# State-space layer: the products on GpSimd moved to VectorE, the table of decay factors to ScalarE

## The chip, the cores and the metric

The kernel runs on one core of one Trainium2 chip. Its time is the device time of one execution in microseconds (us), the median of several runs. A profile of one more execution shows what each engine did: TensorE (PE, with its weight loads as PEld), VectorE (DVE), ScalarE (ACT), GpSimd (POOL) and SyncE (SP), which issues the DMAs.

## What is computed

The reference is one step of a two-layer model on 1280 tokens (1024 latent ones and 256 of context), 1024 wide. Layer 0 projects the normed input to q, k, v and u, runs attention on q, k, v and a bidirectional state-space layer (S5) on u, and projects both back; layer 1 is a Fourier mixer; each layer ends with a SwiGLU feed-forward part. Norms are modulated by shift, scale and gate from a conditioning vector and `w_mod`.

The change lies in S5. For each of 32 groups of 16 channels, two directions and 64 complex states it computes

```
bu = u @ (c * b)                  # complex input weights
x[t] = a * x[t-1] + bu[t]         # complex, diagonal: 64 states
y = Re(x @ c_out);  state = x[last]
```

`x` of both directions is summed into `y`, then GELU and a gated linear unit follow. The last states of the context tokens are an output too.

## The kernel before

The tokens lie along the free dimension: `CH` cuts the 1280 into chunks of 512, 512 and 256, and features lie on the partitions. Every float32 matrix is split into a high and a low part (`wsplit`, L92: a cast on ACT, L96, and a difference on POOL, L97), and a product is three matmuls of such parts (`proj3`, L114, with its matmuls in L123). The normed input is split likewise into `h` (`modulate`, L72 and L73, its differences in turn on DVE and POOL).

S5 works in blocks of eight steps: the 1280 tokens become 160 columns of eight, the recurrence runs over columns with the eighth power of `a`, and what happens inside eight steps is folded into weights. The 32 groups are taken in eight blocks `b` of four. For each block two generators run:

- `s5_prep` (L487) makes the weights. `Bs` and `Bxx` are complex products on tiles of 128x128 (`tmp` is the second product). `cmul` makes `AB` (128x512) and `CA` (128x576), each a product, a second product `ta` and their sum. PE turns `AB` into `Win`. `cpow` (L476) makes the table of rotations `E` by doubling: two products and a sum, twice, for 8, 16, 32 and 64 columns.
- `s5_main` (L562) applies them. PE multiplies `u` by `Win` (L576), ACT copies the result into `v` (L579, L581). `A` and `B` (128x648, four rows of 162) are `v` rotated by `E`, so that the scan is real: `R8` holds the decay factors and zeros where a sequence begins (mask times factor), and two scans on DVE (L596, L597) do the recurrence. Then `A` and `B` rotate back, ACT copies the sums into `x` (L608), POOL copies the last states (L609), and PE makes `y` (L622 to L624).

The helper `tt` emits the products; the profile gives them all the line of the helper: L490 in `s5_prep`, L564 in `s5_main`, L478 in `cpow`. Of the two products of each pair one is on DVE and the other, where its first argument is `G`, on POOL.

`s5_all` (L630) runs `s5_main` of a block in step with `s5_prep` of the next, eight steps per block. `build` (L1163) pulls one such step after each chunk of the projections (`pull`, L1227): four `proj3` for u (L1233), eight for q and k (L1237), then two rounds for v (L1249, matmuls L1257). It also pulls steps of `mods`, which makes the modulation of later sub-layers: 256 KB loads of `w_mod` into two buffers (L1101), matmuls (L1103), a copy on ACT (L1105), a turn on PE (L1114) and a sum on DVE (L1116). `bias_table` (L673, L674) adds small DVE work.

Each engine has one queue that runs in order. The order in the queues is set when the program is built, by a planner with its own costs that takes ready instructions by priority; it can place an instruction ahead of others that the code emits earlier. The scratch tiles of `s5_main` (tag `wm`) share six buffers, those of `s5_prep` (tag `wp`) three.

Of the kernel before, what the change touches and what calls it, by code (L numbers as in the profile page):

```python
# [5 lines left out]
AF=mybir.ActivationFunctionType; ALU=mybir.AluOpType  # L6
# [5 lines left out]
def bank(k,name="p",tag="p"):  # L12
    return k.psum.tile([128,512],F32,tag=tag,bufs=k.banks[tag],name=name)
# [51 lines left out]

def modulate(k, c, A, S, hi, lo, at):
    nc=k.nc; V=nc.vector; c0,n=CH[c]
    for kt in range(KT):
        t=at(n); x=k.xT[kt][:,c0:c0+n]
        if kt%3==1: nc.scalar.activation(t,x,AF.Identity,bias=S(kt,c),scale=A(kt,c))  # L70
        else: V.tensor_scalar(t,x,A(kt,c),S(kt,c),op0=ALU.mult,op1=ALU.add)
        nc.scalar.copy(hi[:,kt],t)  # L72
        (nc.gpsimd if kt%2 else V).tensor_tensor(out=lo[:,kt],in0=t,in1=hi[:,kt],op=ALU.subtract)  # L73

def modnorm(k, c, R, A, S, hi, lo, at):
    nc=k.nc; c0,n=CH[c]
    for kt in range(KT):
        t=at(n)
        if kt%8 in (1,2,4,5,7):
            nc.vector.tensor_tensor(out=t,in0=k.xT[kt][:,c0:c0+n],in1=R,op=ALU.mult)  # L80
            nc.scalar.activation(t,t,AF.Identity,bias=S(kt,c),scale=A(kt,c)); nc.scalar.copy(hi[:,kt],t)
            nc.gpsimd.tensor_tensor(out=lo[:,kt],in0=t,in1=hi[:,kt],op=ALU.subtract)
        else:
            nc.vector.scalar_tensor_tensor(out=t,in0=k.xT[kt][:,c0:c0+n],scalar=A(kt,c),in1=R,op0=ALU.mult,op1=ALU.mult)
            nc.scalar.activation(hi[:,kt],t,AF.Identity,bias=S(kt,c))
            nc.vector.scalar_tensor_tensor(out=lo[:,kt],in0=t,scalar=S(kt,c),in1=hi[:,kt],op0=ALU.add,op1=ALU.subtract)
# [315 lines left out]
LC=162  # L402
# [73 lines left out]
def cpow(e1,e2,re,im,tmp,ms,n):  # L476

    def tt(e,o,i,j,op): e.tensor_tensor(out=o,in0=i,in1=j,op=op)  # L478
    for m in ms:
        br=re[:,:,m:m+1].to_broadcast([128,n,m]); bi=im[:,:,m:m+1].to_broadcast([128,n,m])  # L480
        o=slice(m+1,2*m+1); i=slice(1,m+1); v=tmp[:,:,0:m]
        tt(e2,re[:,:,o],re[:,:,i],br,ALU.mult); tt(e1,v,im[:,:,i],bi,ALU.mult)
        tt(e1,re[:,:,o],re[:,:,o],v,ALU.subtract)
        tt(e2,im[:,:,o],re[:,:,i],bi,ALU.mult); tt(e1,v,im[:,:,i],br,ALU.mult)
        tt(e1,im[:,:,o],im[:,:,o],v,ALU.add)

def s5_prep(k, b, P, io, res):  # L487

    nc=k.nc; V=nc.vector; G=nc.gpsimd; S=nc.scalar
    def tt(e,o,i,j,op): e.tensor_tensor(out=o,in0=i,in1=j,op=op)  # L490
    wt=lambda name,tag="wp",n=3: k.s5b.tile([128,4,LC],F32,tag=tag,bufs=n,name=name)
    xt=lambda sh,name: k.x.tile(sh,F32,tag="x",bufs=8,name=name)
    sm=lambda sh,name,n=1: k.s5b.tile(sh,F32,tag=name,bufs=n,name=name)
    bc=sm([128,4,2,4,16],"bc"); nc.sync.dma_start(bc,io["BC"][b])
    Bst,Bx,Cst,Cx=[bc[:,i] for i in range(4)]
    dd=sm([128,16],"dd"); nc.sync.dma_start(dd,io["dd"][b//2,:,b%2])
    UT=xt([128,1152],"UT"); U=UT[:,0:640].rearrange("p (g c) -> p g c",g=4); Toep=UT[:,640:1152].rearrange("p (g c) -> p g c",g=4)
    gs=lambda t,d: t[:,d*32+4*b:d*32+4*b+4]
    Bs=sm([128,2,5,16],"Bs"); Bxx=sm([128,2,4,16],"Bxx"); tmp=sm([128,2,4,16],"tmp")
    V.memset(Bs[:,:,4],0.0)  # L500
    g2=lambda t: t.rearrange("p (d g) -> p d g",d=2)[:,:,4*b:4*b+4][:,:,:,None].to_broadcast([128,2,4,16])
    tt(V,Bs[:,:,0:4],Bst,g2(P["cr"]),ALU.mult); tt(G,tmp,Bx,g2(P["ci"]),ALU.mult); tt(V,Bs[:,:,0:4],Bs[:,:,0:4],tmp,ALU.add)
    tt(V,Bxx,Bx,g2(P["cr"]),ALU.mult); tmp=sm([128,2,4,16],"tmp"); tt(G,tmp,Bst,g2(P["cn"]),ALU.mult); tt(V,Bxx,Bxx,tmp,ALU.add)
    V.tensor_scalar(Bxx,Bxx,io["sgn"],None,op0=ALU.mult)
    V.tensor_scalar(Cst,Cst,io["sgn"],-1.0,op0=ALU.mult,op1=ALU.mult)
    V.tensor_scalar(Cx,Cx,-1.0,None,op0=ALU.mult)
    yield
    def cmul(o,d,n,sl,u,v):
        p=lambda t: gs(t,d)[:,:,sl][:,:,:,None].to_broadcast([128,4,n,16])
        bb=lambda t: t[:,:,None,:].to_broadcast([128,4,n,16])  # L510
        ta=wt("ta").rearrange("p a c -> p (a c)")[:,0:64*n].rearrange("p (a j h) -> p a j h",a=4,h=16)
        tt(V,o,p(P["PR"]),bb(u),ALU.mult)
        tt(G,ta,p(P["PI"]),bb(v),ALU.mult)
        tt(V,o,o,ta,ALU.add)
    Win=xt([128,2,4,128],"Win"); CA=xt([128,2,4,9,16],"CA")
    def turn(d,AB):
        p=bank(k,tag="s").rearrange("p (a b) -> p a b",a=4)
        for i in range(4): nc.tensor.transpose(p[:,i],AB[:,i].rearrange("p h j -> p (h j)"),k.ident)
        S.copy(Win[:,d],p)
    old=None  # L520
    for d in range(2):

        AB=wt("AB").rearrange("p a c -> p (a c)")[:,0:512].rearrange("p (a h j) -> p a h j",a=4,h=16)
        cmul(AB.rearrange("p a h j -> p a j h"),d,8,slice(0,8) if d==0 else slice(7,None,-1),Bs[:,d,0:4],Bxx[:,d])
        yield
        cmul(CA[:,d],d,9,slice(0,9) if d==0 else slice(8,None,-1),Cst[:,d],Cx[:,d])
        if old is not None: turn(d-1,old)
        old=AB
        yield
    turn(1,old)  # L530

    p=bank(k,tag="s")[:,0:256].rearrange("p (a c) -> p a c",a=2)
    for d in range(2):
        for g in range(4):
            rhs=CA[:,0,g,0:8] if d==0 else CA[:,1,g,1:9]
            nc.tensor.matmul(p[32*g:32*g+32,d],lhsT=Bs[:,d].rearrange("p g h -> p (g h)")[:,16*g:16*g+32],rhs=rhs.rearrange("p j h -> p (j h)"),start=True,stop=True)
    KT=sm([128,15,16],"KT")
    S.copy(KT[:,7:15],p[:,0].rearrange("p (j h) -> p j h",h=16))
    S.copy(KT[:,0:7],p[:,1].rearrange("p (j h) -> p j h",h=16)[:,0:7])
    tt(V,dd,dd,KT[:,7],ALU.add)  # L540
    tt(V,KT[:,7],p[:,1].rearrange("p (j h) -> p j h",h=16)[:,7],dd,ALU.add)
    kd=io["kt_dr"][b]
    nc.sync.dma_start(kd,KT.rearrange("p j h -> p (j h)"))
    for g in range(4):
        a=kd[32*g:32*g+16]
        nc.sync.dma_start(Toep[:,g],bass.AP(tensor=a.tensor,offset=a.offset,ap=[[240,16],[16,8],[1,128]]))
    yield

    E=[wt(f"E{i}","E",4) for i in range(2)]
    ep=P["e"].rearrange("p i (d q) c -> p i d q c",d=2)[:,:,:,2*b:2*b+2]  # L550
    for i in range(2): V.tensor_copy(dq(E[i])[:,:,:,0:9],ep[:,i])
    t=wt("t")
    cpow(V,V,E[0],E[1],t,(8,16),4)
    yield
    cpow(V,G,E[0],E[1],t,(32,64),4)
    for i in range(2): G.tensor_copy(E[i][:,:,129:162],E[i][:,:,0:33])
    res[b]=(Win,CA,U,Toep,E)
    yield

def dq(t): return t.rearrange("p (d q) c -> p d q c",d=2)  # L560

def s5_main(k, b, P, io, res):  # L562
    nc=k.nc; V=nc.vector; G=nc.gpsimd; S=nc.scalar
    def tt(e,o,i,j,op): e.tensor_tensor(out=o,in0=i,in1=j,op=op)  # L564
    wt=lambda name: k.s5b.tile([128,4,LC],F32,tag="wm",bufs=6,name=name)
    Win,CA,U,Toep,E=res.pop(b)
    nc.sync.dma_start(U,io["u_dr"][64*b:64*b+64].rearrange("(g h) s c -> (h s) g c",g=4))
    Vr=[]
    for ri in range(2):
        v=wt("v")  # L570
        for d in range(2):
            p=bank(k,tag="s")
# [10 lines left out]
        Vr.append(v)  # L583
    yield
    R8=wt("R8"); A=wt("A"); B=wt("B")
    r8=P["r8"].rearrange("p (d q) -> p d q",d=2)[:,:,2*b:2*b+2][:,:,:,None].to_broadcast([128,2,2,LC])
    tt(G,dq(R8),k.s5mask[:,None,None,:].to_broadcast([128,2,2,LC]),r8,ALU.mult)
    C,Sn=E
    tt(V,A,Vr[0],C,ALU.mult); tt(G,B,Vr[1],Sn,ALU.mult)
    tt(V,A,A,B,ALU.add)  # L590
    tt(V,B,Vr[1],C,ALU.mult); tt(G,Vr[0],Vr[0],Sn,ALU.mult)
    tt(V,B,B,Vr[0],ALU.subtract)
    for i,t in enumerate((A,B)): V.tensor_copy(dq(t)[:,:,:,0:1],io["s0"][:,i,:,2*b:2*b+2][:,:,:,None])
    yield
# [5 lines left out]
    def put(ri,op):  # L600
# [6 lines left out]
                else: oa,ob=xo[:,:,127::-1],xo[:,:,159:127:-1]  # L607
                S.copy(oa,A[h,q,0:128]); S.copy(ob,A[h,q,129:161])  # L608
        G.tensor_copy(fin[:,ri,:,2*b:2*b+2][:,:,:,None],dq(A)[:,:,:,161:162])  # L609
    tt(V,A,Vr[0],C,ALU.mult); tt(G,B,Vr[1],Sn,ALU.mult)  # L610
    put(0,ALU.subtract)
    yield
    A=wt("A"); B=wt("B"); tt(V,A,Vr[1],C,ALU.mult); tt(G,B,Vr[0],Sn,ALU.mult)
    put(1,ALU.add)
    yield
    yield
# [1 line left out]
    for g0 in (0,2):  # L618
        p=bank(k,tag="s")[:,0:320].rearrange("p (a b) -> p a b",a=2)
# [10 lines left out]
def s5_all(k, P, io):  # L630

    res={}
    for _ in s5_prep(k,0,P,io,res): yield
    for b in range(8):
        m=s5_main(k,b,P,io,res); p=s5_prep(k,b+1,P,io,res) if b<7 else iter(())
        for _ in range(8):
            next(m,None); next(p,None)
            yield
# [808 lines left out]
```

## Time and profile before

| what | before |
|---|---|
| median of 3 runs | 3035.34 us (3032.78 to 3039.38) |
| the profiled execution | 3033.56 us, its span 3031.8 us |
| PE busy | 2709.9 us (89%) |
| DVE busy | 1985.8 us (65%) |
| ACT busy | 1142.1 us (38%) |
| POOL busy | 1065.4 us (35%) |
| DMA | 391.71 MB, 129 GB/s on average |
| granted PE clock over the span | 0.944 |

Busy shares are averages over stages with different limits. S5 runs in the first 15% of the span; its stage is read from views of that stretch. A wait is put down to the instruction that released it last, and a wait of PE stands twice in the profile, at the matmul and at its weight load.

### The profile page before, as it was taken

How to read it: one execution, taken by the hardware profiler on the slowest of the kernel's cores; microseconds unless marked ns; L12 is line 12 of the kernel's file. 1: busy time of each engine (PE TensorE's matmuls, PEld its weight loads, DVE VectorE, ACT ScalarE, POOL GpSimd, SP SyncE). 2: the span in 40 equal slices, each digit the busy share in tenths (PEclk: the TensorE clock that was granted, in tenths of full speed). 3: DMA queues.
4: the chain of work that ended last, by engine and by line, in shares of the span. 5: the costliest groups of instructions: out<-in, count | busy, mean ns of one | idle time of the engine just before them, and what ended most of it. 6: DMA issues, size and time to landing. Idle time of an engine off the chain costs nothing. (4 is left out here: it accounts for less than half of the span.)

```text
span 3031.8 us, 49180 instructions
## 1 busy us (share of the span) xinstructions
PE 2709.9 (89%) x18042; PEld 2471.6 (82%) x18042; DVE 1985.8 (65%) x3769; ACT 1142.1 (38%) x2419; POOL 1065.4 (35%) x913
## 2 busy tenths in 40 slices
PE   4778889888998999999999997996799999989997
PEld 1556666766797999999999986985699999989996
DVE  8876740787668766564667748377947454666674
ACT  3332332565445333333422223244433333443232
POOL 3665534554224311111433344343411111243334
PEclk7888999999998999999999998997899999999998
DMA  6245567344433333333643432431323332554421
GB/s 223 84 121 154 162 189 212 82 117 117 158 106 116 102 128 121 120 134 112 222 140 132 143 107 70 153 106 56 120 82 130 117 114 88 168 198 154 159 79 70
DMA packets 283706, 391.71 MB, mean 129 GB/s; under 512 B 34236, under 2 KB 196156, under 8 KB 283464
## 3 DMA queue, kind: packets, MB, share of 16 engines
q1 hardware_dynamic: 265320, 330.74, 34.1%
q10 hardware_dynamic: 15552, 53.09, 5.1%
q0 software_dynamic: 2592, 4.73, 0.6%
q8 instruction: 142, 2.33, 0.3%
q14 instruction: 100, 0.82, 0.1%
HBM read 291.96 MB, written 96.50 MB: 128 GB/s over the span
## 5 line engine op out<-in xcount | busy, mean ns | idle before, releaser
L276 PE MATMUL p<-op,w 128*128 128x320 f32 x8688 | 1342.9, 315 | 83.5 <-ACT w L160 24.0
L276 PEld LDWEIGHTS p<-op,w 128*128 128x128 f32 x8688 | 1312.2, 192 | 105.0 <-ACT w L160 26.9
L160 POOL TENSOR_TENSOR w<-raw,w 128x512 fp32r<-128x512 f32 (+1 forms) x230 | 321.4, 1400 | 973.8 <-ACT w L160 902.2
L160 ACT CAST w<-raw 128x512 fp32r<-128x512 f32 (+1 forms) x396 | 240.0, 607 | 283.8 <-PE p L276 182.6
L276 PE MATMUL p<-op,e 128*128 128x320 f32 x1728 | 274.3, 312 | 16.4 <-ACT e L160 11.4
L276 PEld LDWEIGHTS p<-op,e 128*128 128x128 f32 x1728 | 258.3, 189 | 22.8 <-ACT e L160 11.9
L177 DVE TENSOR_TENSOR raw<-raw 128x512 f32<-128x512 f32 (+1 forms) x228 | 159.4, 699 | 165.5 <-POOL w L160 104.5
L320 DVE SCALAR_TENSOR_TENSOR xt<-p,mod,xt 128x320 f32<-128x320 f32 (+2 forms) x432 | 193.4, 471 | 101.4 <-PE p L276 99.7
L283 DVE TENSOR_TENSOR e<-p,e 128x320 f32<-128x320 f32 x264 | 127.0, 486 | 168.3 <-PE p L276 144.0
L160 DVE TENSOR_TENSOR w<-raw,w 128x512 fp32r<-128x512 f32 (+1 forms) x166 | 123.3, 743 | 120.5 <-ACT w L160 117.6
L123 PE MATMUL p<-h,wh 128*128 128x512 f32 (+1 forms) x576 | 185.8, 394 | 18.0 <-ACT h L72 11.6
L160 POOL TENSOR_TENSOR e<-raw,e 128x384 fp32r<-128x384 f32 x72 | 79.0, 1097 | 260.2 <-ACT e L160 260.2
L123 PEld LDWEIGHTS p<-h,wh 128*128 128x128 f32 x576 | 109.0, 201 | 49.9 <-ACT h L72 12.7
L1348 PE MATMUL p<-o,w 128*128 128x320 f32 x768 | 115.6, 312 | 3.6 <-ACT w L160 3.6
L1348 PEld LDWEIGHTS p<-o,w 128*128 128x128 f32 x768 | 114.6, 191 | 4.0 <-ACT w L160 3.8
L160 ACT CAST e<-raw 128x384 fp32r<-128x384 f32 x96 | 48.7, 512 | 179.9 <-PE p L276 113.6
L309 DVE TENSOR_TENSOR e<-e 128x320 f32<-128x320 f32 (+1 forms) x216 | 110.1, 561 | 0.8 <-DMA hT<-e 0.4
L123 PE MATMUL p<-h,wl 128*128 128x512 f32 (+1 forms) x288 | 110.5, 384 | 0.0
L767 POOL TENSOR_TENSOR P<-P,l 128x384 f32<-128x384 f32 (+1 forms) x80 | 68.7, 860 | 104.4 <-DVE l L764 65.1
L332 DVE TENSOR_TENSOR op<-op 128x320 fp32r<-128x320 f32 x120 | 84.1, 726 | 16.9 <-ACT op L332 16.9
L160 ACT CAST w<-st 128x512 fp32r<-128x512 f32 (+1 forms) x76 | 44.6, 587 | 132.0 <-PE p L276 129.6
L103 PE MATMUL p<-ac 128*128 128x512 f32 (+1 forms) x432 | 92.0, 367 | 2.3 <-DVE ac L380 2.3
(397 smaller groups left out, 4520.6 us busy)
## 6 DMA issues: line engine op xcount, KB each, us to landing
hT<-e SPq DMA_DIRECT2D x324, 160.0 KB
op<-hT ACTq DMA_DIRECT2D x108, 480.0 KB
mw<-in_w_mod_dram SPq DMA_DIRECT2D x160, 256.0 KB
raw<-in_wg_dram SPq DMA_DIRECT2D x104, 256.0 KB
raw<-in_wu_dram SPq DMA_DIRECT2D x104, 256.0 KB
raw<-in_wd_dram SPq DMA_DIRECT2D x96, 192.0 KB
xt<-x_dr SPq DMA_DIRECT2D x24, 640.0 KB
xt<-in_x_dram SPq DMA_DIRECT2D x16, 640.0 KB
```

The lines of the kernel that those rows point to most:

```text
L103: k.nc.tensor.matmul(p,lhsT=w,rhs=x,start=i==0,stop=i==n-1)
L123: k.nc.tensor.matmul(ps[c],lhsT=w[i][:,kt],rhs=h[c][j][:,4*pc+kt],start=pc==0 and kt==0 and m==0,stop=pc==1 and kt==3 and m==2)
L160: k.nc.scalar.copy(hi,src); eng.tensor_tensor(out=lo,in0=src,in1=hi,op=ALU.subtract)
L177: def tt(o,x,y,op=ALU.subtract): V.tensor_tensor(out=o,in0=x,in1=y,op=op)
L276: k.nc.tensor.matmul(p,lhsT=w[i][:,kt],rhs=x[j][:,kt],start=P in (1,2,5) and n==0,stop=n==3*kn-1,skip_group_check=P!=2); n+=1
L283: def add(o): V.tensor_tensor(out=o,in0=p,in1=o,op=ALU.add)
L309: def tt(o,x,y): V.tensor_tensor(out=o,in0=x,in1=y,op=ALU.subtract)
L320: x=k.xT[d][:,c0:c0+n]; V.scalar_tensor_tensor(out=x,in0=p[:,o:o+n],scalar=self.gate(d,c),in1=x,op0=ALU.mult,op1=ALU.add)
L332: nc.scalar.copy(hi,r); (nc.vector if self.nq%3 else nc.gpsimd).tensor_tensor(out=lo,in0=r,in1=hi,op=ALU.subtract)
L767: nc.gpsimd.tensor_tensor(out=a,in0=a,in1=l.to_broadcast(a.shape),op=ALU.mult)
L1348: nc.tensor.matmul(ps[r],lhsT=w[x][:,kt],rhs=o[t][y][:,4*pc+kt,HALF*r:HALF*r+HALF],start=pc==0 and kt==0 and n==0,stop=pc==1 and kt==3 and ...
```

## The change

All products and sums of two operands in S5 go to DVE. `R8` is no longer one product on POOL over 128x648: for each of its four rows ACT scales the mask (162 elements) by that row's factor. The copies of `E` and of the last states and the memsets stay on POOL, as does everything outside S5.

```diff
--- before.py
+++ after.py
@@ -499,8 +499,8 @@
-    tt(V,Bs[:,:,0:4],Bst,g2(P["cr"]),ALU.mult); tt(G,tmp,Bx,g2(P["ci"]),ALU.mult); tt(V,Bs[:,:,0:4],Bs[:,:,0:4],tmp,ALU.add)
-    tt(V,Bxx,Bx,g2(P["cr"]),ALU.mult); tmp=sm([128,2,4,16],"tmp"); tt(G,tmp,Bst,g2(P["cn"]),ALU.mult); tt(V,Bxx,Bxx,tmp,ALU.add)
+    tt(V,Bs[:,:,0:4],Bst,g2(P["cr"]),ALU.mult); tt(V,tmp,Bx,g2(P["ci"]),ALU.mult); tt(V,Bs[:,:,0:4],Bs[:,:,0:4],tmp,ALU.add)
+    tt(V,Bxx,Bx,g2(P["cr"]),ALU.mult); tmp=sm([128,2,4,16],"tmp"); tt(V,tmp,Bst,g2(P["cn"]),ALU.mult); tt(V,Bxx,Bxx,tmp,ALU.add)
@@ -510,7 +510,7 @@
         tt(V,o,p(P["PR"]),bb(u),ALU.mult)
-        tt(G,ta,p(P["PI"]),bb(v),ALU.mult)
+        tt(V,ta,p(P["PI"]),bb(v),ALU.mult)
         tt(V,o,o,ta,ALU.add)
@@ -552,7 +552,7 @@
-    cpow(V,G,E[0],E[1],t,(32,64),4)
+    cpow(V,V,E[0],E[1],t,(32,64),4)
@@ -583,12 +583,13 @@
     R8=wt("R8"); A=wt("A"); B=wt("B")
-    r8=P["r8"].rearrange("p (d q) -> p d q",d=2)[:,:,2*b:2*b+2][:,:,:,None].to_broadcast([128,2,2,LC])
-    tt(G,dq(R8),k.s5mask[:,None,None,:].to_broadcast([128,2,2,LC]),r8,ALU.mult)
+    r8=P["r8"].rearrange("p (d q) -> p d q",d=2)[:,:,2*b:2*b+2][:,:,:,None]
+    for d in range(2):
+        for q in range(2): S.activation(R8[:,2*d+q],k.s5mask,AF.Copy,scale=r8[:,d,q])
     C,Sn=E
-    tt(V,A,Vr[0],C,ALU.mult); tt(G,B,Vr[1],Sn,ALU.mult)
+    tt(V,A,Vr[0],C,ALU.mult); tt(V,B,Vr[1],Sn,ALU.mult)
     tt(V,A,A,B,ALU.add)
-    tt(V,B,Vr[1],C,ALU.mult); tt(G,Vr[0],Vr[0],Sn,ALU.mult)
+    tt(V,B,Vr[1],C,ALU.mult); tt(V,Vr[0],Vr[0],Sn,ALU.mult)
     tt(V,B,B,Vr[0],ALU.subtract)
@@ -607,10 +608,10 @@
-    tt(V,A,Vr[0],C,ALU.mult); tt(G,B,Vr[1],Sn,ALU.mult)
+    tt(V,A,Vr[0],C,ALU.mult); tt(V,B,Vr[1],Sn,ALU.mult)
     put(0,ALU.subtract)
     yield
-    A=wt("A"); B=wt("B"); tt(V,A,Vr[1],C,ALU.mult); tt(G,B,Vr[0],Sn,ALU.mult)
+    A=wt("A"); B=wt("B"); tt(V,A,Vr[1],C,ALU.mult); tt(V,B,Vr[0],Sn,ALU.mult)
     put(1,ALU.add)
```

## Rows read from the trace of the kernel before

**Rows 1.** Windows: stretch, length; busy (count) of PE, PEld, DVE, ACT, POOL; clock, DMA.
```profile
66.00:220.00 154.00, 112.36 (x687) 85.80 (x687) 125.50 (x197) 52.20 (x137) 100.43 (x92) 0.84 0.34 97
220.00:455.00 235.00, 203.69 (x1584) 147.77 (x1582) 151.58 (x260) 75.87 (x212) 115.50 (x128) 0.92 0.57 168
455.00:525.00 70.00, 66.28 (x371) 46.62 (x371) 7.09 (x11) 17.60 (x22) 29.70 (x25) 1.00 0.70 201
```
**Rows 2.** Waits of PE from 66 to 220 us: total us, times, longest.
```profile
PE p L623 <- ACT x L608: 18.5, 2, 12.1
...
PE p L1103 <- DVE mod L1116: 7.4, 1, 7.4
```
**Rows 3.** Waits of PE from 220 to 455 us.
```profile
PE p L1103 <- DMA mw<-in_w_mod_dram: 15.6, 12, 3.5
PE p L1103 <- DVE mod L1116: 5.2, 2, 2.8
PE p L1103 <- ACT mr L1105: 4.5, 1, 4.5
PE p L1114 <- ACT mr L1105: 3.5, 2, 2.3
```
**Rows 4.** Windows right after six stalls of PE: the first and the last of six.
```profile
146.40:151.00 4.60, 4.60 (x17) 4.31 (x18) 3.39 (x19) 3.66 (x11) 1.32 (x6) 0.53 0.45 139
...
437.00:441.00 4.00, 4.00 (x31) 3.78 (x32) 0.00 (x0) 3.65 (x2) 0.00 (x0) 0.57 0.66 209
```
**Rows 5.** Groups by line on POOL, 58 to 450 us: busy, mean ns | idle before.
```profile
L564 POOL TENSOR_TENSOR B<-v,E 128x648 f32<-128x648 f32 x24 | 46.6, 1950 | 34.8 <-DVE v L597 34.8
...
L97 POOL TENSOR_TENSOR wl<-raw,wh 128x512 fp32r<-128x512 f32 x26 | 39.1, 1507 | 34.3 <-ACT wh L96 32.0 <-DVE Bs L490 2.3
...
L490 POOL TENSOR_TENSOR tmp<-bc,s5ci 128x128 f32<-128x128 f32 x8 | 4.5, 556 | 9.4 <-DMA bc<-in_BC_dram 9.4
```
**Rows 6.** Timeline of POOL: start us, duration us, what.
```profile
269.25 1.37 POOL L97 TENSOR_TENSOR wl<-raw,wh 128x512 fp32r<-128x512 f32 x1 [0.54 <-ACT wh L96]
```
**Rows 7.** Timeline of DVE at the same time.
```profile
269.42 1.25 DVE L478 TENSOR_TENSOR t<-E 128x32 f32<-128x32 f32 x1
270.59 0.18 DVE L478 TENSOR_TENSOR E<-E 128x32 f32<-128x32 f32 x1
```
**Rows 8.** Lines L490 and L564 on DVE: shortest/median/longest ns, first and last start us.
```profile
L490 DVE TENSOR_TENSOR AB<-s5PR,Bs x16: 1065/1910/2312, 73.0 to 373.1; 128x512 f32<-128x512 f32 x16
...
L490 DVE TENSOR_TENSOR CA<-s5PR,bc x16: 743/746/751, 93.1 to 393.2; 128x576 f32<-128x576 f32 x16
...
L564 DVE TENSOR_TENSOR B<-v,E x8: 810/834/835, 132.2 to 422.7; 128x648 f32<-128x648 f32 x8
```
**Rows 9.** Timeline of DVE: products of `cpow` with POOL idle or elsewhere.
```profile
228.08 0.29 DVE L478 TENSOR_TENSOR t<-E 128x128 f32<-128x128 f32 x1
...
229.77 0.42 DVE L478 TENSOR_TENSOR t<-E 128x256 f32<-128x256 f32 x1
```
**Rows 10.** Groups by line on DVE, 66 to 455 us.
```profile
L564 DVE TENSOR_TENSOR A<-A,B 128x648 f32<-128x648 f32 x24 | 33.6, 1418 | 33.1 <-POOL B L564 33.1
L564 DVE TENSOR_TENSOR A<-v,E 128x648 f32<-128x648 f32 x24 | 28.5, 1211 | 29.8 <-ACT v L581 29.8
L490 DVE TENSOR_TENSOR AB<-s5PR,Bs 128x512 f32<-128x512 f32 x16 | 26.3, 1643 | 0.3
L490 DVE TENSOR_TENSOR AB<-AB,ta 128x512 f32<-128x512 f32 x16 | 25.9, 1622 | 7.8 <-POOL ta L490 7.8
...
L596 DVE TENSOR_TENSOR_SCAN v<-R,A 128x648 f32<-128x648 f32 x8 | 12.0, 1498 | 0.0
```
**Rows 11.** Timeline of DVE: first and last piece of one block's scan part.
```profile
246.58 0.83 DVE L564 TENSOR_TENSOR A<-v,E 128x648 f32<-128x648 f32 x1 [5.39 <-ACT v L581]
...
260.75 2.94 DVE L564 TENSOR_TENSOR A<-A,B 128x648 f32<-128x648 f32 x2 [1.47 <-POOL B L564]
```
**Rows 12.** Groups by line on ACT, 58 to 450 us.
```profile
L608 ACT COPY x<-A 64x256 f32<-64x256 f32 (+1 forms) x128 | 35.3, 322 | 73.3 <-DVE A L564 72.4
```

## The prediction

> **What bounds the kernel now.** I read the page first: the chain that ended last lies in the feed-forward part, but it reaches back only to the second half of the span, so it says nothing about the stage that is changed. The state-space layer (S5) is found by its lines, L490, L478 and L564, which run from about 70 to 430 us [rows 8]. Next I read the windows by stage [rows 1]. From 66 to 220 us VectorE (DVE) is busy for 125.5 of 154 us and TensorE (PE) for 112.4 at a granted clock of 0.84. From 220 to 455 us PE is busy for 204 of 235 us and DVE for 152. Behind them, from 455 us, PE is busy for 66 of 70 us at full clock, so what PE wins before 455 us is passed on.
>
> Then the waits of PE. Up to 220 us, 18.5 us are spent at L623, the S5 output product, whose x copies ScalarE (ACT) makes from a DVE sum, and 7.4 us on L1116, a small DVE sum of the modulation that stands in DVE's queue among S5's [rows 2]. After 220 us there are 5.2 us on the same L1116 and 4.5 + 3.5 us on L1105, an ACT copy behind those x copies; 15.6 us are spent on the loads of w_mod [rows 3]. S5 therefore holds PE for 25.9 + 13.2 = 39.1 us.
>
> [...]
>
> **Why S5 is late.** Its products are split over DVE and GpSimd (POOL). POOL needs 1.95 us on average for a product of 128x648 [rows 5], DVE 0.83 where nothing disturbs it [rows 8]. And the two do not really run side by side. POOL's L97 ran from 269.25 to 270.62 us [rows 6]; the DVE product of 128x32 that starts at 269.42 takes 1.25 us and ends at 270.67, right behind it, while the next one of that size takes 0.18 [rows 7]. A DVE operation on two SBUF tensors was held until the POOL operation had ended.
>
> **The change, step by step.** Nine groups of POOL instructions go; the largest is B with 46.6 us, the smallest tmp (ci) with 4.5 [rows 5]; the nine sum to 148.1 us, nearly all of it in the first two windows, in which POOL is busy for 216 [rows 1]. L97's 39.1 us stay, with the h split, memsets and small copies.
>
> Added on DVE, 112 instructions in eight blocks: 32 products of 128x648 at 0.834 (B<-v,E is the same operation, already on DVE) make 26.7 us; 16 of 128x576 at 0.746 make 11.9 [rows 8]; 16 of 128x512 have no undisturbed row with these layouts: below, 0.66 by scaling the 576 one, above, 1.07, the least of AB, which writes across its tile; ta is written in order, so I take 0.66, 10.6 us (17.1 at most) [rows 8]; 32 of 128x128 at 0.29, 9.3 us, and 16 of 128x256 at 0.42, 6.7 us [rows 9]. Together 65.2 us as durations.
>
> Neighbours overlap a little: the operation that ends at 270.67 us has its follower starting at 270.59 [rows 7]. With 0.08 us off each of 112 the queue grows by 56 us, of which 3.0 per block lie in the scan part (s5_main) and 4.0 in the preparation. [...]
>
> Removed from DVE's time: waits for POOL's result, 33.1 us in front of A<-A,B and 7.8 in front of AB<-AB,ta; and holding. Over their undisturbed durations [rows 8] the four largest groups spend 33.6 - 20.0, 28.5 - 20.0, 26.3 - 17.1 and 25.9 - 17.1 us, together 40.3 [rows 10]. Two thirds of POOL's time leaves (148 of 216), so I let two thirds of this go, 27 us; none of it is the lower bound, and all of it, with smaller groups that I don't count, the upper.
>
> Per block, scan part: + 3.0 - 33.1/8 - (22.1 x 2/3)/8 = + 3.0 - 4.1 - 1.8 = - 2.9 us. A single block shows the same: from the first A at 246.58 to the end of the last sum at 263.69 us it takes 17.1 us [rows 11]; twelve operations of 0.834, two scans of 1.5 [rows 10] and two small copies (0.1 each by the starts in rows 7) make 13.2, so - 3.9. Preparation: + 4.0 - 7.8/8 - (18.2 x 2/3)/8 = + 4.0 - 1.0 - 1.5 = + 1.5 us.
>
> R8, the decay table, becomes four ACT instructions per block of 162 elements. The nearest row is ACT's copy, 0.32 us [rows 12]: 32 x 0.32 = 10.3 us on ACT, which spends 72 us waiting for DVE's A. It is needed only at the scan, seven DVE operations later. I cost it at nothing; if ACT's queue brings it late, 1.3 us per block, 10 in all, is the other end.
>
> What hides the rest. After 220 us DVE has 83 us idle, so the preparation's + 1.5 is covered and only the scan part counts: five blocks at 2.9 to 3.9 us make 14.5 to 19.5, and PE can gain there at most its S5 stalls of 13.2 and half the clock loss, 7.2, together 20.4. I take 16. Before 220 us DVE is busy for four fifths of the time and has little cover, so both parts count: three blocks at - 1.4 make 4, and with some clock given back 6. The sum is - 22 us. Bounds: 0 if nothing of the holding goes and ACT is late, - 54 (39.1 + 14.5) if every S5 stall ends.
>
> POOL's queue gets shorter, and L97 no longer stands behind products that wait for DVE, so the weight splits come earlier. Next late in the second stretch are the w_mod loads, two buffers deep.
>
> The profiled execution took 3033.56 us (span 3031.8), 1.8 below the median of 3035.34. 3033.6 - 22 = 3011.6, on the median's scale 3013 us.
>
> **Rivals.** (A) All S5 stalls end, because the remaining lateness falls under PE's other work. For it: the 18.5 us at L623 are two stalls only [rows 2]. Against it: before 220 us DVE is near full. 3035.3 - 54 = 2981 us.
>
> (B) No change: PE reaches each w_mod product earlier and waits there instead. For it: 15.6 us of such waits, and loads that can't be issued before PE has read the buffer. Against it: they are spread over twelve waits, and DMA is at 0.57 [rows 1, 3]. 3031 to 3039 us.
>
> (C) Slower: DVE becomes the bound. The mechanism is that the long DVE durations don't come from the moved POOL work (L97, DMA or layout cause them) and stay. Then + 65.2 - 41 = + 24 us on a queue which is full up to 220 us and on which L1116 and the h splits of the first projection wait too: 3059 us. It decides from the point where the holding that goes is less than 15 us (56 - 41). For it: part of the holding is L97's. Against it: the pair of rows 6 and 7, where the same size takes 1.25 and 0.18 us.
>
> The order in the queues is a planner's, made at build: L1116 stands among S5's work, though that is emitted elsewhere. With other operations it may place S5's products at other points of PE's queue; that is part of each case's width.
>
> **Chances.** Forecast, 2990 to 3027 us: 0.62. (A) 0.16. (B) 0.10. (C) 0.12. From a measured kernel 0.2% (6 us) is about what can be told from no change. Faster 0.78, same 0.10, slower 0.12. The range takes in (A) and (B) and leaves out (C): 2979 to 3038 us.
>
> **What would show it.** A<-A,B at a mean near 0.85 us instead of 1.42 and no DVE wait for POOL at L564; AB near 1.1; DVE's busy time up to 455 us about the same as now, with less idle time; PE's wait at L623 below 10 us and the clock from 66 to 220 us above 0.86; the w_v products (L1257) starting some 20 us earlier than at 455 us; everything behind them equally long. Wrong would be: A<-A,B still above 1.2 us; an L623 wait that grows; or a later stage whose length changes by more than a few us.

## The result, and the profile after

The changed kernel takes 2998.55 us (median of 4 runs, 2994.13 to 3000.1), the kernel before on the same chip 3035.3 us: ratio 0.9879, 95% interval 0.9867 to 0.9891. That is 36.8 us less, where 22 were forecast. The profiled execution took 2994.13 us, its span is 2992.4 us. One run of e5 below (3725.86 us) and one of the kernel before that was timed beside it (5654.81 us) took far longer than the others and are left out of every comparison. Lines behind `R8` stand one further down than before (L608 is now L609).

Where the time went is read at the landmark that the prediction chose, the first weight load of the w_v products, which ends S5's stretch. The rows, of before and of after, give the first and the last start.

```profile
L1257 PEld LDWEIGHTS p<-wh,h x160: 186/188/192, 455.5 to 522.6; 128*128 128x128 f32 x160
```

```profile
L1258 PEld LDWEIGHTS p<-wh,h x160: 186/188/192, 411.1 to 479.1; 128*128 128x128 f32 x160
```

The stretch got 44.4 us shorter. Windows of before over it, and up to 250 us:

```profile
66.00:250.00 184.00, 138.82 (x900) 105.17 (x904) 144.10 (x238) 61.58 (x165) 115.74 (x113) 0.84 0.37 105
...
66.00:455.50 389.50, 316.37 (x2276) 233.75 (x2276) 277.08 (x457) 128.07 (x349) 216.43 (x219) 0.89 0.48 140
```

And of after, over the same work and over the two stages of [rows 1]:

```profile
66.00:220.00 154.00, 134.37 (x896) 101.42 (x896) 142.88 (x293) 66.09 (x181) 56.22 (x53) 0.92 0.42 120
220.00:455.00 235.00, 212.75 (x1642) 148.29 (x1637) 137.54 (x282) 83.05 (x213) 63.90 (x58) 0.96 0.66 194
```

```profile
66.00:411.10 345.10, 305.51 (x2257) 222.76 (x2258) 276.45 (x566) 134.16 (x377) 104.76 (x99) 0.93 0.53 153
```

Three things are to be seen. PE's idle time in the stretch fell from 389.5 - 316.4 = 73.1 us to 345.1 - 305.5 = 39.6, by 33.5; its busy time for nearly the same matmuls (2257 against 2276 records) fell by 10.9, with the granted clock up from 0.89 to 0.93. The two make the 44.4. DVE's busy time did not move, 277.1 and 276.5 us, though 109 more instructions ran on it. And the lead was won early: by 220 us PE has started 896 matmuls, which it had reached only by 250 us before (900). Busy time times clock, as an estimate of the work, says the same: 134.4 x 0.92 = 124 against 138.8 x 0.84 = 117.

The waits of PE, first from 66 to 220 us and then to 411 us, answer to [rows 2, 3].

```profile
PE p L1104 <- DMA mw<-in_w_mod_dram: 4.4, 3, 2.9
...
PE p L623 <- ACT Win L519: 2.8, 1, 2.8
PE p L1104 <- DVE mod L1117: 2.8, 1, 2.8
```

```profile
PE p L1104 <- DMA mw<-in_w_mod_dram: 9.3, 16, 1.3
PE p L123 <- POOL wl L97: 7.8, 2, 4.9
PE p L624 <- ACT x L609: 1.1, 1, 1.1
```

The products that waited for the x copies, L623 before, are L624 now; what is L623 now was L622. So the 18.5 us on the x copies are gone up to 220 us, and 1.1 us are left behind it; the loads of w_mod cost 13.7 us in place of 15.6, and one wait is new: 7.8 us on L97, the low half of the weights on POOL.

DVE's groups up to 440 us (they answer to [rows 10]):

```profile
L564 DVE TENSOR_TENSOR B<-v,E 128x648 f32<-128x648 f32 x32 | 29.6, 924 | 2.2 <-ACT v L581 2.1
L564 DVE TENSOR_TENSOR A<-A,B 128x648 f32<-128x648 f32 x24 | 21.8, 908 | 0.1
L564 DVE TENSOR_TENSOR A<-v,E 128x648 f32<-128x648 f32 x24 | 20.6, 860 | 12.2 <-ACT v L581 12.2
L490 DVE TENSOR_TENSOR AB<-s5PR,Bs 128x512 f32<-128x512 f32 x16 | 19.9, 1246 | 0.1
L490 DVE TENSOR_TENSOR AB<-AB,ta 128x512 f32<-128x512 f32 x16 | 19.1, 1195 | 0.0
L478 DVE TENSOR_TENSOR E<-E,t 128x32 f32<-128x32 f32 (+3 forms) x64 | 18.6, 291 | 0.0
```

No group waits for POOL any more, and A<-A,B went from a mean of 1.42 to 0.91 us. The two largest groups that are left on POOL:

```profile
L97 POOL TENSOR_TENSOR wl<-raw,wh 128x512 fp32r<-128x512 f32 x32 | 61.5, 1924 | 173.0 <-ACT wh L96 162.6 <-PE p L1104 10.2 <-DMA UT<-u_dr 0.2
L610 POOL COPY fin<-A 128x4 f32<-128x4 f32 x16 | 27.8, 1759 | 59.5 <-DVE A L564 59.5
```

The second of these groups in the kernel before, from 58 to 450 us, and then the decay table after:

```profile
L609 POOL COPY fin<-A 128x4 f32<-128x4 f32 x16 | 10.1, 629 | 7.1 <-DVE A L564 7.0
```

```profile
L588 ACT ACTIVATE R<-mk,s5r 128x162 f32<-128x162 f32 x32 | 12.4, 442 | 0.0
```

L97 takes 1.92 us where it took 1.51 [rows 5], and a copy of four columns 1.76 where it took 0.63: what stays on POOL became slower. Behind S5 about 5 us are given back in the profiled executions (spans of 3031.8 and 2992.4 us, 39.4 of the 44.4; by the medians 36.8). The attention that follows starts at 480.8 instead of 524.3 us and ends at 747.3 instead of 786.5: 4.3 us longer.

```profile
L754 PE MATMUL S<-ch,qs x64: 393/497/795, 524.3 to 786.5; 128*128 128x512 f32 x64
```

```profile
L755 PE MATMUL S<-ch,qs x64: 392/497/794, 480.8 to 747.3; 128*128 128x512 f32 x64
```

### The profile page after: what moved, and what is told of

Same layout as the page of the kernel before. It is cut to its first block, busy times and chain, and to the rows that moved or that the text cites. A ratio compares the mean times of both kernels' runs of the same rounds, so it can differ in the third digit from the quotient of the medians.

```text
span 2992.4 us, 49124 instructions
## 1 busy us (share of the span) xinstructions
PE 2698.2 (90%) x18042; PEld 2463.3 (82%) x18042; DVE 1985.4 (66%) x3881; ACT 1151.3 (38%) x2451; POOL 951.0 (32%) x793
## 5 line engine op out<-in xcount | busy, mean ns | idle before, releaser
L97 POOL TENSOR_TENSOR wl<-raw,wh 128x512 fp32r<-128x512 f32 x44 | 77.0, 1752 | 201.0 <-ACT wh L96 190.6
```

The source lines that it names most:

```text
L97: nc.gpsimd.tensor_tensor(out=l,in0=raw,in1=h,op=ALU.subtract)
```

## The experiments

All are timed against the kernel before on their own chip. "S5's end" is the first start of the w_v loads, as above.

| run | what | median us | ratio to before, 95% | S5's end |
|---|---|---|---|---|
| after | the change | 2998.55 | 0.9867 to 0.9891 | 411.1 |
| e1_lock | after + unread POOL products | 3058.04 | 1.0049 to 1.0095 | 475.5 |
| e2_write | after + POOL memsets | 3011.65 | 0.9890 to 0.9947 | 430.4 |
| e3_main | scan part alone | 3003.92 | 0.9868 to 0.9920 | 422.9 |
| e4_prep | preparation alone | 3029.49 | 0.9970 to 0.9993 | 443.9 |
| e5_fin_dve | after, fin on DVE | 2995.10 | 0.9844 to 0.9881 | 404.9 |
| e6_fin_act | after, fin on ACT | 2977.53 | 0.9793 to 0.9824 | 394.6 |
| e7_r8_pool | after, R8 on POOL | 2989.67 | 0.9826 to 0.9862 | 402.2 |
| e8_after_again | after, with e5 to e7 | 2992.58 | 0.9847 to 0.9884 | 409.6 |
| e9_fin_act_r8_pool | e6 and e7 together | 2982.95 | 0.9798 to 0.9846 | 402.9 |
| e10_low_on_dve | e6 + 24 of L97 on DVE | 2984.72 | 0.9804 to 0.9851 | 397.6 |

**Does POOL's reading hold DVE?** The theory has two parts. A hand-off is DVE's wait for a result of POOL; holding is the longer time that a DVE operation takes while POOL runs. The two kernels give back to POOL about the time that the change took from it, in work whose result (`k.jk`, a scratch half of a tile) nobody reads. In the first it reads two SBUF inputs. In the second it writes: 117 us of memsets, with one product of four elements ahead of each row (24, together 16 us). DVE and PE have the work of the kernel after, in the same numbers and in the same order. `caf` is a view of the tile `CA`, `jf` one of a table of `E`.

```diff
 # e1: in s5_prep, twice per block, and in s5_main, once per block
...
+        for _ in range(3): tt(G,k.jk,caf[64:128,d,0:512],caf[64:128,d,0:512],ALU.mult)
...
+    for _ in range(6): tt(G,k.jk,jf(C),jf(Sn),ALU.mult)
 # e2: at the same places
...
+        tt(G,k.jk[:,0:4],caf[64:128,d,0:4],caf[64:128,d,0:4],ALU.mult)
+        for _ in range(7): G.memset(k.jk,0.0)
...
+    tt(G,k.jk[:,0:4],jf(C)[:,0:4],jf(Sn)[:,0:4],ALU.mult)
+    for _ in range(14): G.memset(k.jk,0.0)
...
```

> The changed kernel with 96 extra products on POOL (64 partitions x 512, six in each scan part and six in each preparation) whose results nobody reads; the output is unchanged, and the queues of PE, DVE and ACT stand in the same order as in the changed kernel. Holding (a POOL operation that reads SBUF holds DVE's two-input operations): POOL gets about 100 us of work back, A<-A,B on DVE rises from 0.91 us to 1.2 or more, and 20 to 30 of the 36.8 us are given back: 3018 to 3030 us. Hand-off (the gain came from waits for POOL's slower half of each pair, which is not restored here): no more than 3003 us. Order (the planner's other order made the gain; it is kept here): no more than 3003 us.

> The same as the first, but POOL's extra work is 224 memsets that only write SBUF (each row of them behind one product of four elements), again read by nobody and with the queues of PE, DVE and ACT in the same order. If only POOL operations that read SBUF hold DVE: A<-A,B stays near 0.91 us and the time at 2996 to 3004 us. If any POOL operation does, or if POOL's full queue (L97 behind the extra work) is what costs: as in the first, 3015 us or more. Hand-off and order: no more than 3003 us.

Windows of the first and of the second, from 66 us to S5's end:

```profile
66.00:475.50 409.50, 317.31 (x2257) 230.88 (x2258) 348.59 (x567) 134.50 (x377) 249.01 (x195) 0.89 0.44 128
```

```profile
66.00:430.40 364.40, 306.81 (x2258) 224.11 (x2259) 276.66 (x566) 134.40 (x377) 241.62 (x347) 0.92 0.50 145
```

POOL is busy for 144 and 137 us longer than after (104.8). With the reading, DVE needs 72.1 us more for the same instructions; with the writing, 0.2. So about half a microsecond of DVE is lost per microsecond of the added reading, and next to none for the writing. The groups show it at the instruction (E<-E,t had 0.29 and A<-A,B 0.91 us), again the first and the second:

```profile
L478 DVE TENSOR_TENSOR E<-E,t 128x32 f32<-128x32 f32 (+3 forms) x64 | 34.1, 533 | 0.0
...
L566 DVE TENSOR_TENSOR A<-A,B 128x648 f32<-128x648 f32 x24 | 26.1, 1087 | 0.1
```

```profile
L567 DVE TENSOR_TENSOR A<-A,B 128x648 f32<-128x648 f32 x24 | 21.8, 910 | 0.1
...
L478 DVE TENSOR_TENSOR E<-E,t 128x32 f32<-128x32 f32 (+3 forms) x64 | 20.0, 312 | 0.1
```

The reading costs more than the change gained, 59.5 us over the kernel after where 20 to 30 were expected, with next to no hand-off (DVE waits 2.7 us for POOL in it). A<-A,B came to 1.09 us only, short of the 1.2 expected; the small products of `E` lost more, E<-E,t alone 15.5 us. The theory of the holding is confirmed; hand-offs or another order alone don't explain the gain. With the hand-offs gone, the order kept and POOL reading again, S5 ends at 475.5 us, 20 us later than before the change.

The writing came out between its two expectations, 13 us above the kernel after, and costs in another way. L97 comes later behind the memsets in POOL's queue (12.1 us of PE's waits in place of 7.8), and PE waits 16.2 us in two places for loads of `UT`. These are late through L97 as well. In SyncE's queue a load of weights (L94) waited until L97 had read the buffer, 57.7 us in nine waits; both late loads of `UT` stand right behind such an L94, the first issued at 119.40 us, 0.9 us after an L94 that had waited 6.3 us. SyncE's waits for L97 up to S5's end, with the memsets and in the kernel after:

```profile
SPq L94 <- POOL wl L97: 57.7, 9, 18.1
```

```profile
SPq L94 <- POOL wl L97: 29.2, 8, 13.9
```

The profile of e2 is of its longest run (3019.8 us), so its S5's end stands at the late side.

**Which part?** The scan part alone and the preparation alone, on the kernel before. The planner's order of PE's queue is another one in each of them.

```diff
 # e3: s5_main as after; s5_prep as before
-    tt(V,A,Vr[0],C,ALU.mult); tt(G,B,Vr[1],Sn,ALU.mult)
+    tt(V,A,Vr[0],C,ALU.mult); tt(V,B,Vr[1],Sn,ALU.mult)
...
 # e4: s5_prep as after; s5_main as before
-        tt(G,ta,p(P["PI"]),bb(v),ALU.mult)
+        tt(V,ta,p(P["PI"]),bb(v),ALU.mult)
...
```

> One part of the change alone: s5_main's products on DVE and its table on ACT, the preparation as before. By the working of the prediction this part shortens a block by 2.9 us and more and the preparation lengthens it by 1.5: 3005 to 3012 us, that is at least two thirds of the 36.8. If holding is what counts, POOL keeps 75 us of the preparation's work and AB's mean on DVE stays above 1.4 us. If the preparation's share is the larger one: above 3020 us.

> The other part alone: the preparation's products on DVE, s5_main as before with its waits for B on POOL. By the prediction's step (+1.5 us per block): 3033 to 3042 us. By holding, which frees the preparation's DVE operations, and if the two parts add up: 36.8 less what the main part gives, 3020 to 3030 us.

S5's end comes 32.6 us earlier with the scan part, 11.6 with the preparation; together that is 44.2, as with both (44.4). Per block they are worth 4.1 and 1.5 us. Of the total, 30 us are the scan part's, whose time lies 1 us below its range, and 5 the preparation's, in the range by holding, whose kernel gives back 4.4 us in the attention. Each leaves the other's contention standing; first a group of the scan part alone, then one of the preparation alone:

```profile
L490 DVE TENSOR_TENSOR AB<-AB,ta 128x512 f32<-128x512 f32 x16 | 25.8, 1610 | 10.2 <-POOL ta L490 10.2
```

```profile
L564 DVE TENSOR_TENSOR A<-A,B 128x648 f32<-128x648 f32 x24 | 37.2, 1568 | 18.7 <-POOL B L564 18.7
```

**What is next late?** The new wait on L97 and the copies of `fin`, which stand ahead of it in POOL's queue, led to these four. The last is the kernel after once more.

```diff
 # e5, e6: fin on DVE, on ACT
-        G.tensor_copy(fin[:,ri,:,2*b:2*b+2][:,:,:,None],dq(A)[:,:,:,161:162])
+        V.tensor_copy(fin[:,ri,:,2*b:2*b+2][:,:,:,None],dq(A)[:,:,:,161:162])
+        S.copy(fin[:,ri,:,2*b:2*b+2][:,:,:,None],dq(A)[:,:,:,161:162])
 # e7: the table back on POOL
...
-        for q in range(2): S.activation(R8[:,2*d+q],k.s5mask,AF.Copy,scale=r8[:,d,q])
+    tt(G,dq(R8),k.s5mask[:,None,None,:].to_broadcast([128,2,2,LC]),r8,ALU.mult)
```

> The kernel after, with the copy of the last column of each part (fin) on VectorE in place of GpSimd. In the kernel after these 16 copies hold GpSimd's in-order queue for 27.8 us and keep it waiting for VectorE's A for 59.5 us, and the low half of the weights (L97) is queued behind them: TensorE waits 7.8 us for it, in 2 places. Theory (the end of GpSimd's queue is the next bound): both waits go, 16 copies of some 0.1 to 0.3 us come to VectorE, and it runs 3 to 8 us below the kernel after: 2990 to 2996. Rival (the two waits are made up by matmuls that the planner has in hand): 2997 to 3002, no difference.

> The same copy on ScalarE in place of GpSimd. Theory (the wait for VectorE's A, not the copy, is what costs): the wait of 59.5 us moves into ScalarE's in-order queue, ahead of the modulation, the evictions and the high half of the weights, so TensorE's waits on ScalarE grow: 3000 to 3012. Rival (ScalarE is waiting for that A anyway, because its next instruction is the copy of x that reads the same A): as with the copy on VectorE, 2990 to 2998.

> The kernel after, with the table of decay factors back on GpSimd (8 instructions of 128x648) in place of 32 small ones on ScalarE. Theory (it was off the path; what it holds of VectorE is 8 times at most its own 1.5 us): 0 to 8 us above the kernel after, 2998 to 3006. Rival (ScalarE's 12.4 us for it stood on the path, ahead of the copy of v for which VectorE waits 12.2 us): 3 to 10 us below the kernel after, 2988 to 2995.

> The kernel after as it stands, on the same chip as the three kernels above, to compare them with: 2994 to 3002 by what it took the first time. If it comes out elsewhere, the three are compared with this run and not with the first.

With fin on DVE the time does not move (2995.10 beside 2992.58, whose runs reach from 2991 to 3002). My theory of POOL's queue is not borne out: the fin copies are gone from POOL, yet PE still waits 4.0 us for L97 (8.4 in e8), and the 4.7 us by which S5 ends earlier don't show in the total. The timelines tell why L97 is late without them. First after, around the longer of its two stalls: POOL from 380.06 us, DVE's row of products at that time, and PE.

```profile
380.06 7.50 POOL L97 TENSOR_TENSOR wl<-raw,wh 128x512 fp32r<-128x512 f32 x2 [22.23 <-ACT wh L96]
...
383.04 0.82 DVE L564 TENSOR_TENSOR A<-A,B 128x648 f32<-128x648 f32 x1
383.78 0.82 DVE L564 TENSOR_TENSOR B<-v,E 128x648 f32<-128x648 f32 x1
384.63 1.79 DVE L564 TENSOR_TENSOR A<-A,B 128x648 f32<-128x648 f32 x1
385.78 0.79 PE L123 MATMUL p<-h,wl 128*128 128x512 f32 x1 [4.89 <-POOL wl L97]
```

Then the kernel with fin on DVE, where no fin copy is ahead of L97 either:

```profile
327.65 4.15 POOL L97 TENSOR_TENSOR wl<-raw,wh 128x512 fp32r<-128x512 f32 x1 [17.50 <-ACT wh L96]
```

Two L97, whose median is 1.30 us, take 7.5, one takes 4.15. DVE's products ran back to back at 0.82 us, undisturbed, for as long as L97 stood, until one took 1.79. By these rows the holding went both ways: a DVE queue without gaps kept POOL out. After this stall the clock was low: 0.50 from 386 to 391 us of the kernel after.

With fin on ACT the time falls by 15 us, to 2977.53, the best of all and below both expectations. The 16 copies take 0.197 us each there, and ACT does not pay for the wait: it is idle for 0.3 us before them, and for 28.5 us before the x copies of the same `A`, where it was 31.7 in the kernel after. But the copy itself is worth little (DVE did it in 0.30). What differs is the stretch from 295 to 400 us; first fin on ACT, then the kernel after run beside it:

```profile
295.00:400.00 105.00, 97.81 (x791) 70.15 (x791) 65.09 (x128) 45.12 (x122) 21.92 (x21) 1.00 0.68 203
```

```profile
295.00:400.00 105.00, 89.35 (x695) 64.82 (x694) 66.26 (x129) 34.91 (x107) 34.72 (x26) 0.90 0.58 169
```

PE's wait for L97 is 1.0 us here instead of 8.4, and the clock stays at 1.00. A shorter queue on POOL is not what it takes. With the table back on POOL (e7) POOL is busy for 112.0 us up to S5's end, in e8 for 107.4, and PE waits only 0.8 us for L97; with both edits (e9) it does not wait for L97 at all. Both end S5 at 402 to 403 us, some 8 us behind fin on ACT. So that wait is not all of the 15 us. The planner's order of PE's queue differs in every variant (e5, e6, e7, e9, e10; e8 has that of the kernel after); what the order is worth was not tested and stays open. The table back on POOL takes 2989.67, in its rival's range, but its runs overlap with those of the kernel after: no difference can be told.

**Do they add up, and does the remaining contention cost anything?** Two more: both edits together, and fin on ACT with the low half of the weights of u, q and k on DVE.

```diff
 # e10, on top of fin on ACT: proj3 hands DVE to the helper for the difference
-    nc.gpsimd.tensor_tensor(out=l,in0=raw,in1=h,op=ALU.subtract)
+    (low or nc.gpsimd).tensor_tensor(out=l,in0=raw,in1=h,op=ALU.subtract)
```

> The kernel after with fin on ScalarE and the table of decay factors back on GpSimd, the two edits that each came out below it alone (by 15 and by 3 us). If each takes away its own cost, they add up: 2970 to 2977. Rival (both worked through the same stall, TensorE's wait for the low weights of L97, or through the order that the planner then chose): nothing is added, 2976 to 2990.

> The kernel with fin on ScalarE (2977.5 us), and in the projections of u, q and k the low half of the weights (L97, 24 instructions of 128x512) on VectorE too in place of GpSimd. Theory (VectorE and GpSimd hold each other: L97 takes 1.93 us on average where it needs 1.28, and VectorE waits behind it): 24 products of 0.7 us are added to VectorE, 17 us, and the holding that L97 causes goes, about as much, so its products come down to their undisturbed durations (the 128x32 ones of E to 0.18) and the time stays within 2970 to 2980. Rival (VectorE is full up to 220 us and its in-order queue now brings the low weights late): TensorE's waits at L123 for them grow above 10 us, 2985 to 3000.

Nothing is added: 2982.95, 5 us above fin on ACT alone, as the rival had it. It ran on another chip, and the intervals of the two ratios overlap, so the 5 us themselves are not shown. The second takes 2984.72 us, in the gap between the two expectations. Its trace shows what the holding by L97 was worth:

```profile
L97 DVE TENSOR_TENSOR wl<-raw,wh x24: 665/679/693, 63.6 to 377.7; 128x512 fp32r<-128x512 f32 x24
```

```profile
L564 DVE TENSOR_TENSOR A<-A,B 128x648 f32<-128x648 f32 x24 | 19.8, 823 | 0.0
...
L490 DVE TENSOR_TENSOR AB<-s5PR,Bs 128x512 f32<-128x512 f32 x16 | 18.3, 1144 | 0.0
```

The rotations are now at their undisturbed duration, the products of `E` of 128x32 at the expected 0.18 us, and PE waits only 1.2 us for the low halves. Up to S5's end DVE is busy for 268.8 us where it was 277.3 with fin on ACT, though 16 us of differences came to it. S5 still ends at 397.6 us, not before the 394.6 of fin on ACT: what contention was left on DVE does not show in the end of the stage. This profile is 4 us above its kernel's median, so the 3 us between the ends tell nothing.

## Why the prediction was right, and where its size was off

The direction and the mechanism hold: waits for POOL (40.9 us) and holding by POOL (A<-A,B from 1.42 to 0.91 us) go, PE's idle time goes with them (73.1 to 39.6 us), the clock rises (0.89 to 0.93), DVE's busy time stays (277.1 and 276.5 us). The sum was 15 us short. In the stage itself it was short by 22 (44.4 against 22); that the total came nearer is the loss behind S5, which was not forecast: luck, not working. By its steps:

- **Added on DVE, 65.2 us.** Measured about 72.5 by durations: 22.2 (24 of the 32 B<-v,E) + 6.6 (v) + 26.1 (the two ta) + 12.0 (cpow) + 5.6 (tmp). Some are still held by L97: one B<-v,E beside it takes 1.85 us, where the median is 0.83. ta of 128x512 took 0.75 us on average in the kernel after, near the 0.66 taken and far from the 1.07. AB, which writes across its tile, stays at 1.14 even undisturbed (e10), two thirds more than ta there, whose inputs are laid out alike but which is written in order (median 0.69). The 0.42 of [rows 9] was read while POOL ran a product of its own, not with POOL idle; e10 has 0.42 for that size too, so the price stands.
- **Waits removed, 40.9 us.** All gone, and the smaller ones with them.
- **Holding removed, 27 us: the step that failed.** The four groups alone fell by 32.9 (A<-A,B 11.8, A<-v,E 7.9, AB 6.4 and 6.8) [rows 10]; I had taken two thirds of their excess (its four differences sum to 40.1, not 40.3, and those of AB to 18.0, not 18.2), and four fifths went. And the groups that I did not count lost another 13.9: E<-E,t 23.2 to 18.6, t<-E 13.9 to 10.1, the h split 12.5 to 9.0, the second scan 13.8 to 11.8 us. That makes 46.8. The busy time of the stretch says more: it stayed at 277 us with about 72.5 added, so about 73 went from the rest, overlap of neighbours included. e1 has about the same rate: 72.1 for 144 us more of POOL, where the change took 148 us of work from it. POOL's busy time fell by only 111.6, since L97 and the copies of `fin` became longer.
- **Scan part, - 2.9 to - 3.9 per block.** The part alone brought S5's end forward by 4.1 per block, just beyond the far end.
- **Preparation, + 1.5 per block.** Wrong in sign: - 1.5. Put on top of the scan part (from e3 to after) it left DVE's busy time in the stretch where it was, 278.3 and 276.5 us, where the step has 20 us more, and took away a wait for ta of 10.2 us: more holding went than counted, on the small operations too (E<-E,t from 24.4 to 18.6 us). Alone it also cut the scan part's waits for B from 33.1 [rows 10] to 18.7 us, which the step left out.
- **R8 on ACT at nothing.** Not contradicted: 0.442 us each, not 0.32, but putting it back on POOL makes no difference that can be told.
- **Before 220 us - 6, after it - 16.** The other way round: PE is some 30 us ahead by 220 us, and 14 more are won to S5's end. With both parts better than costed, the stage where DVE was nearest to full gained most, not least.
- **Ceiling, 39.1 + 14.5 us (rival A).** Nearly reached in the stage: 33.5 of idle time and 10.9 of clock. No run shows the 14.5 us of clock loss, nor the half of it, 7.2, that the forecast takes after 220 us; the runs showed a clock of 0.53 and 0.57 after two stalls [rows 4], and PE's busy time in the stretch 10.9 us shorter, with the clock up from 0.89 to 0.93. Rival A was nearer in mechanism than my forecast; its total was missed by the new wait on L97 (7.8 us) and the 5 us behind S5. The prediction had the weight splits come earlier by POOL's shorter queue; instead L97 was held by DVE (1.92 us on average where it took 1.51), and PE, which had no such wait before, waits for it.
- **Everything behind equally long.** Wrong by those 5 us. At the start of the attention the clock is 0.66 (480 to 501.5 us) where it was 0.76 (523.5 to 545). Over all kernels timed here the attention's span, first to last L755, lies between 262.2 and 269.9 us and follows no edit; why it varies stays open.
- **Rival B** (PE only waits for w_mod instead) falls: 13.7 us against 15.6. **Rival C** (the long durations stay) falls with A<-A,B at 0.91 us and with the pair e1 and e2 (its 3059 us adds 65.2 where its own threshold counts 56). The clock above 0.86 up to 220 us (0.92) and the wait at L623, now L624, below 10 us (1.1) came as said; A<-A,B stayed a little above 0.85 and AB above 1.1.

## What to carry to other kernels

Price a POOL operation with two SBUF inputs not at zero because it runs "beside" DVE, but at what DVE loses while it runs, here about half of its duration (72.1 us for 144), and count this for every small DVE operation of the stretch, not for the four largest groups. After such a move look at what stayed on POOL: here it was held out by the fuller DVE (L97 from 1.51 to 1.92 us), and TensorE waited for it, directly (7.8 us) or, in e2, through loads that stood behind it in SyncE's queue (16.2 us). And with a planner behind the queues, differences of 5 to 15 us between near variants are not to be read as the price of the edited instruction.

## What was not expected of the hardware

The holding showed in both directions and lasted over several DVE operations: POOL's copy of 128x4 took 1.76 us on average in the kernel after (0.63 before), on ACT 0.197, and a single L97 up to 5.67 where the median of all 44 is 1.30. ACT's copies of it were not held at all (0.196 to 0.198 us over 16, e6). And 117 us of memsets on POOL left DVE's busy time unchanged within 0.2 us (276.7 beside 276.5).
